# The seam between two layers: four expert blocks in the tile-by-tile end, and the third tile's norm at a lower priority

## The chip, the core and the metric

The kernel runs on one core of a Trainium2 chip. The core has a tensor engine (PE) for matmuls and transposes, VectorE (DVE), ScalarE (ACT) and GpSimd (POOL) for elementwise work, and SyncE (SP), which here only issues DMA transfers. Each engine takes its instructions in a fixed order and waits on semaphores for the others. Matmuls write PSUM, which has 8 banks here; everything else lies in SBUF. The metric is the device time of one execution in microseconds (us); the time before is the median of three runs.

## What is computed

Two layers of a hybrid trunk act on 256 latent tokens and 256 context tokens of width 1024. In each layer one input projection feeds four mixers (a convolution over 31 taps, neighbourhood attention, a Hyena convolution and a Mamba-2 scan), an output projection and a norm follow, then an expert layer (PEER) and a second norm. Cut to the part that matters:

```
for l in range(DEPTH):                                   # DEPTH = 2
    y, yc = mixer_sublayer(x * (1 + sc1) + sh1, xc * (1 + sc1c) + sh1c, ...)
    x = layer_norm(alpha * x + g1 * y, ln1_g[l], ln1_b[l])
    x = layer_norm(alpha * x + g2 * peer(x * (1 + sc2) + sh2, ...), ln2_g[l], ln2_b[l])
    # the same for the context xc, in layer 0 only
```

`peer` weighs the rows of a table of 16384 experts (`peer_v`) for every token and sums them. `mixer_sublayer` of layer 1 begins with `h @ w_in`, and h needs the second norm of layer 0: that step from one layer to the next is the seam.

## The kernel before

**Tiles and blocks.** Tokens stand in tiles of 128. In layer 0 three tiles (0 and 1 latent, 2 context; `DT`) go through a dense form of the expert sum: the 16384 experts are 128 blocks of 128, and for every block the tile's weights (w, made into wh and wl) are multiplied with the block's rows of the value table (v_hi and v_lo). Each product is three matmuls (`mm3`, L144 to L146: hi*hi, hi*lo, lo*hi), for two halves of 512 columns; so a block has 3 x 2 x 3 = 18 matmuls, and the sums lie in six PSUM banks (`ov`). The fourth tile (the other context tile, `GT`) goes another way (gathered rows) and is done before the seam.

**A block's values.** `values` issues one 512 KB transfer into a raw buffer of pool `vp` (SP, v_raw, L1294), casts it on ACT (v_hi, L140) and takes the rest on DVE (v_lo, L141). `VB[0]` is 2: two raw buffers, and two each of v_hi and v_lo. So a block's transfer can be issued once v_lo of two blocks earlier has read the raw buffer, and its v_hi can be written once PE is done with the values of two blocks earlier.

**The end of the expert layer.** The main loop runs the blocks one by one, all three tiles each. The last `NE` blocks are the tail: tile after tile, half after half, with the blocks innermost, so that a tile's sums are complete before the next tile's begin. Then `combine` multiplies a tile's sums with a gate (cm, L1317), adds them to the residual (L1318, one half on DVE, one on POOL), takes statistics (L1319), works out the scale ln_rs (DVE L297, L299; POOL L300 to L302) and applies it on ACT (x_n, L1333). `to_hT` transposes x_n on PE in 2 x 4 steps (xT, L792), scales it into h (ACT L798, DVE L800) and splits that into hT (ACT cast L140, DVE rest L141), the right-hand side of layer 1's projections.

**What comes next.** Layer 1 loads blocks of weights (`load_w`: w_raw; w_hi on ACT L140; w_lo on POOL L141; three buffers each of w_hi and w_lo) and multiplies each with hT (`projT`, banks `pj`, 24 matmuls a block). The first ten blocks use 256 columns, tiles 0 and 1, the later ones with 512 all four tiles. The convolution's input is written to a padded buffer upad (L378), which POOL has cleared (MEMSET, L349); its 31 taps for each of two halves run on DVE (L366 the first, L368 the other 60). The Hyena part's short convolutions (hv: ACT L343, DVE L344, L345) end in a product (L389), which PE transposes (ut, L404). Later the step sizes of the scan are worked out on DVE (L443 to L458, ending with av), which PE needs for pc (L463); then follow the rope products (rot on PE L484; kr, qr, r1k on DVE L486 to L488).

**What sets the order.** A scheduler orders every engine's instructions when the kernel is built, by the dependences, its own estimate of the times and a priority number: work written later has a higher number and goes later, where it can. `low(n)` adds n to that number for what is inside; the taps have low(3000). `tc.issue_after` holds instructions behind a named one. On the chip each engine then runs its list in order.

Of the kernel before, what the change touches and what calls it, by code (L numbers as in the profile page):

```python
# [31 lines left out]
HB2 = 4  # L32
# [9 lines left out]
XB = (96, 100, 104, 108)  # L42
VD = (10, 1)
UM = ((0, 2, 4, 6, 7), (0, 1, 2, 3, 4, 5, 6, 7))
NE = 2
WHB = (4, 5)
WB = 3
PW = (1, 1)
# [38 lines left out]
def tile_hybrid_diffusion(ctx: ExitStack, tc: tile.TileContext, I: dict, out: bass.AP):  # L87
    nc = tc.nc
    V, S, G, T = nc.vector, nc.scalar, nc.gpsimd, nc.tensor
# [723 lines left out]
    prep = {}  # L813
# [33 lines left out]
    for l in range(2):  # L847
# [426 lines left out]
        with ExitStack() as vst:  # L1274
# [17 lines left out]
            def values(bl, p, n, eng=G):  # L1292
                raw = mk(vp, [128, D], tag="v_raw", bufs=VB[l])
                late["v", bl] = nc.sync.dma_start(raw, I["v"][l, bl])  # L1294
                hi = mk(p, [128, D], F32R, tag="v_hi", bufs=n)
                lo = mk(p, [128, D], F32R, tag="v_lo", bufs=n)
                split(raw, hi, lo, eng)
                return hi, lo
# [75 lines left out]
                nc.gpsimd.dma_start(xd[t], x_)  # L1374

            gat = gathered() if GT else iter(())
            last = 128 - NE
            for st in range(UBl, last + UBl):
                if st < 128:
                    u_stage(st)  # L1380
# [11 lines left out]
            ws, vs_ = [], []  # L1392
            for bl in range(last, 128):
                ws.append(weights(bl))
                if bl < 127 or l:
                    vs_.append(values(bl, vp, VB[l], V))
            rg_s.close()
            xp_s = ExitStack()
            x_n = mk(pool("xp", stack=xp_s, side="right"), [128, len(DT), D], name="x_n")
            fle = ExitStack()  # L1400
            if l == 0:
                vs_.append(values(127, pool("vep", stack=fle, side="right"), 1, V))
            end = tc.issue_after(late["v", 127 - VD[l]].ins)
            end.__enter__()
            for i, t in enumerate(DT):
# [20 lines left out]
            end.__exit__(None, None, None)  # L1426
            if l == 0:
                prep.clear()
                prep.update(raw=(pool("fl", stack=fle, side="right"), 3))
            for i, t in enumerate(DT):  # L1430
                for hh in range(2):
                    with tc.issue_after(prev.ins):
                        for j in range(NE):
                            ins = accum(last + j, i, *ws[j], *vs_[j], (hh,))
                    prev = ins
                if i == len(DT) - 1 - FI and l == 0:
                    fill_to(1, FX)
                lst = mk(gp, [128, 1, 2, 6], tag="ln_st")
                r = x_n[:, i, :]
                combine(t, r, gb[t // 2], lambda hh: pacc[i, hh], lst, lnr if l else None)  # L1440
                if l == 0:
                    to_hT([t], lambda t: x_n[:, DT.index(t), :], lnc, hT, gp, hb=HB2)
            fle.close()
        dn.close()
    xp_s.close()
# [116 lines left out]
```

## Time and profile before

| | |
|---|---|
| median of three runs (lowest to highest) | 2890.71 us (2876.44 to 2892.68) |
| the profiled execution, its own time | 2900.05 us |
| its span, mean granted PE clock | 2898.2 us, 0.964 |
| PE busy | 2676.9 us (92%) |
| DVE busy | 2015.2 us (70%) |
| ACT busy | 1122.6 us (39%) |
| POOL busy | 620.0 us (21%) |

All times in the rows below are microseconds from the start of that execution's span. A row gives the start, the length, the engine, the line of the kernel and the operation with the tiles it writes and reads; in brackets stands how long the engine was idle before it and what ended the wait. PE's matmuls overlap: each lasts 0.39 us while the next one starts 0.23 us later. The seam lies between about 1790 and 1940 us.

### The profile page before, as it was taken

Reading aid. Unit: us, or ns where it says so; the run is one execution under the profiler, and the core shown is the slowest. Engines: PE = TensorE matmul, PEld = TensorE weight load, DVE = VectorE, ACT = ScalarE, POOL = GpSimd, SP = SyncE. Lnnn points to the kernel's source line nnn. Section 1 sums busy time; section 2 is a strip of 40 time slices with the busy share of each in tenths; the row PEclk is TensorE's granted clock in tenths of the full one; section 3 lists DMA queues with packets and bytes.
Section 4 is the critical chain, followed back from the end, with each engine's and each line's share of the span. In section 5 each row is a group of like instructions: output and inputs, shape, how many; then the busy total and the mean of one; then the engine's idle time right before and its main releaser. Section 6 shows DMA issues by size and latency. Waiting matters only on the chain. (4 is left out here: it accounts for less than half of the span.)

```text
span 2898.2 us, 41581 instructions
## 1 busy us (share of the span) xinstructions
PE 2676.9 (92%) x15550; PEld 2281.7 (79%) x15550; DVE 2015.2 (70%) x4273; ACT 1122.6 (39%) x1762; POOL 620.0 (21%) x439
## 2 busy tenths in 40 slices
PE   6797899888899999999899999699999999999997
PEld 3674566668889998888788887675889999999986
DVE  4956447968587787877767745875789765555556
ACT  2233531225433333333333333434336544444443
POOL 2233000025423444444334301530000000000000
PEclk8899999989999999999999999799999999999999
DMA  7122333346798999989889835326338976766655
GB/s 258 58 92 95 124 139 102 122 148 248 250 334 310 325 324 321 320 303 307 307 311 312 271 100 182 113 88 218 131 121 306 348 223 203 218 216 200 195 189 197
DMA packets 241838, 625.06 MB, mean 216 GB/s; under 512 B 22424, under 2 KB 104794, under 8 KB 236004
## 3 DMA queue, kind: packets, MB, share of 16 engines
q1 hardware_dynamic: 201156, 475.05, 49.4%
q0 software_dynamic: 40480, 147.36, 14.2%
q8 instruction: 122, 2.00, 0.3%
q14 instruction: 80, 0.66, 0.1%
HBM read 573.04 MB, written 49.30 MB: 215 GB/s over the span
## 5 line engine op out<-in xcount | busy, mean ns | idle before, releaser
L146 PE MATMUL au<-hT,u_lo 128*128 128x384 f32 (+1 forms) x1952 | 612.2, 314 | 19.4 <-POOL u_lo L141 13.8
L144 PE MATMUL au<-hT,u_hi 128*128 128x384 f32 (+1 forms) x1952 | 613.6, 314 | 4.0 <-DVE slT L1212 3.0
L145 PE MATMUL au<-hT,u_hi 128*128 128x384 f32 (+1 forms) x1952 | 610.7, 313 | 0.0
L145 PE MATMUL ov<-v_lo,wh 128*128 128x512 f32 x1280 | 505.5, 395 | 30.0 <-DVE v_lo L141 29.9
L146 PE MATMUL ov<-v_hi,wl 128*128 128x512 f32 x1280 | 501.0, 392 | 0.0
L144 PE MATMUL ov<-v_hi,wh 128*128 128x512 f32 x1280 | 461.9, 393 | 5.8 <-ACT wh L140 5.8
L140 ACT CAST u_hi<-u_raw 128x1024 fp32r<-128x1024 f32 x244 | 256.1, 1050 | 492.7 <-PE au L145 327.7
L146 PEld LDWEIGHTS au<-hT,u_lo 128*128 128x128 f32 x1952 | 371.5, 190 | 24.3 <-POOL u_lo L141 14.8
L144 PEld LDWEIGHTS au<-hT,u_hi 128*128 128x128 f32 x1952 | 371.9, 191 | 12.2 <-DVE slT L1212 3.4
L141 DVE TENSOR_TENSOR u_lo<-u_raw,u_hi 128x1024 fp32r<-128x1024 f32 x220 | 268.4, 1221 | 159.5 <-ACT u_hi L140 159.3
L145 PEld LDWEIGHTS au<-hT,u_hi 128*128 128x128 f32 x1952 | 371.7, 190 | 7.3
L141 DVE TENSOR_TENSOR v_lo<-v_raw,v_hi 128x1024 fp32r<-128x1024 f32 x255 | 312.4, 1226 | 77.7 <-ACT v_hi L140 77.0
L140 ACT CAST v_hi<-v_raw 128x1024 fp32r<-128x1024 f32 x256 | 268.0, 1047 | 112.5 <-DMA v_raw<-in_v_dram 85.2
L145 PEld LDWEIGHTS ov<-v_lo,wh 128*128 128x128 f32 x1280 | 242.0, 189 | 85.1 <-DVE v_lo L141 41.4
L140 ACT CAST wh<-act 128x384 fp32r<-128x384 f32 (+1 forms) x256 | 116.9, 459 | 447.1 <-PE ov L145 444.0
L144 PEld LDWEIGHTS ov<-v_hi,wh 128*128 128x128 f32 x1280 | 242.7, 190 | 50.6 <-ACT wh L140 6.1
L146 PEld LDWEIGHTS ov<-v_hi,wl 128*128 128x128 f32 x1280 | 241.9, 189 | 49.7
L1344 POOL DMA_INDIRECT grow<-in_vg_dram,eu x128 | 179.2, 1400 | 220.7 <-DVE accg L1357 172.0
L1357 DVE SCALAR_TENSOR_TENSOR accg<-grow,ag,accg 128x1024 f32<-128x1024 f32 x127 | 162.8, 1282 | 90.0 <-DMA grow<-in_vg_dram,eu 89.3
L1344 POOL DMA_INDIRECT grow<-in_ug_dram,eu x128 | 163.4, 1276 | 260.9 <-DVE grow L1348 225.9
L141 DVE TENSOR_TENSOR wl<-act,wh 128x384 fp32r<-128x384 f32 (+1 forms) x256 | 125.0, 490 | 101.8 <-ACT wh L140 100.5
L1348 DVE SCALAR_TENSOR_TENSOR grow<-grow,h2n 128x1024 f32<-128x1024 f32 x128 | 155.9, 1221 | 55.3 <-DMA grow<-in_ug_dram,eu 55.2
(834 smaller groups left out, 4039.1 us busy)
## 6 DMA issues: line engine op xcount, KB each, us to landing
u_raw<-in_uT_dram SPq DMA_DIRECT2D x256, 512.0 KB
v_raw<-in_v_dram SPq DMA_DIRECT2D x256, 512.0 KB
Gd<-stg SPq DMA_DIRECT2D x40, 1024.0 KB
gt<-Gd SPq DMA_DIRECT2D x80, 512.0 KB
wa_raw<-in_w_ada_dram SPq DMA_DIRECT2D x76, 512.0 KB
w_raw<-in_w_in_t_dram SPq DMA_DIRECT2D x44, 512.0 KB
w_raw<-in_wq_dram SPq DMA_DIRECT2D x32, 512.0 KB
w_raw<-in_w_ada_dram SPq DMA_DIRECT2D x20, 512.0 KB
```

Source lines behind the costliest of these rows:

```text
L140: S.copy(hi, src)
L141: late["V" if eng in (None, V) else "G"] = (eng or V).tensor_tensor(lo, src, hi.bitcast(F32), ALU.subtract)
L144: T.matmul(o, lh, rh, start=first, stop=False)
L145: T.matmul(o, lh, rl, start=False, stop=False)
L146: return T.matmul(o, ll, rh, start=False, stop=last)
L1344: nc.gpsimd.indirect_dma_start(out=r, out_offset=None, in_=I[tab], in_offset=bass.IndirectOffsetOnAxis(ap=eu[:, i:i + 1], axis=0))
L1348: V.scalar_tensor_tensor(r, r, 1.0, h2n, op0=ALU.mult, op1=ALU.mult, accum_out=ag[:, i:i + 1])
L1357: V.scalar_tensor_tensor(accg, r, ag[:, i:i + 1], accg, op0=ALU.mult, op1=ALU.add)
```

## The change

`NE` becomes a pair: four tail blocks in layer 0, two in layer 1 as before. Of these four, the hi and lo parts of the last two (blocks 126 and 127) lie in pool `vep`, which has two buffers now where it had one for block 127; their raw parts stay in `vp`. Pool `fl` is declared with two buffers where it had three; no tile is taken from it. And for the third tile of layer 0 `combine` and `to_hT` stand in `low(2000)`.

```diff
@@ -42,7 +42,7 @@
 XB = (96, 100, 104, 108)
 VD = (10, 1)
 UM = ((0, 2, 4, 6, 7), (0, 1, 2, 3, 4, 5, 6, 7))
-NE = 2
+NE = (4, 2)
 WHB = (4, 5)
 WB = 3
 PW = (1, 1)
@@ -1374,7 +1374,7 @@
                 nc.gpsimd.dma_start(xd[t], x_)
 
             gat = gathered() if GT else iter(())
-            last = 128 - NE
+            last = 128 - NE[l]
             for st in range(UBl, last + UBl):
                 if st < 128:
                     u_stage(st)
@@ -1392,14 +1392,16 @@
             ws, vs_ = [], []
             for bl in range(last, 128):
                 ws.append(weights(bl))
-                if bl < 127 or l:
+                if bl < 126 or l:
                     vs_.append(values(bl, vp, VB[l], V))
             rg_s.close()
             xp_s = ExitStack()
             x_n = mk(pool("xp", stack=xp_s, side="right"), [128, len(DT), D], name="x_n")
             fle = ExitStack()
             if l == 0:
-                vs_.append(values(127, pool("vep", stack=fle, side="right"), 1, V))
+                vep = pool("vep", stack=fle, side="right")
+                for bl in (126, 127):
+                    vs_.append(values(bl, vep, 2, V))
             end = tc.issue_after(late["v", 127 - VD[l]].ins)
             end.__enter__()
             for i, t in enumerate(DT):
@@ -1426,20 +1428,21 @@
             end.__exit__(None, None, None)
             if l == 0:
                 prep.clear()
-                prep.update(raw=(pool("fl", stack=fle, side="right"), 3))
+                prep.update(raw=(pool("fl", stack=fle, side="right"), 2))
             for i, t in enumerate(DT):
                 for hh in range(2):
                     with tc.issue_after(prev.ins):
-                        for j in range(NE):
+                        for j in range(NE[l]):
                             ins = accum(last + j, i, *ws[j], *vs_[j], (hh,))
                     prev = ins
                 if i == len(DT) - 1 - FI and l == 0:
                     fill_to(1, FX)
                 lst = mk(gp, [128, 1, 2, 6], tag="ln_st")
                 r = x_n[:, i, :]
-                combine(t, r, gb[t // 2], lambda hh: pacc[i, hh], lst, lnr if l else None)
-                if l == 0:
-                    to_hT([t], lambda t: x_n[:, DT.index(t), :], lnc, hT, gp, hb=HB2)
+                with low(2000 if l == 0 and t == DT[-1] else 0):
+                    combine(t, r, gb[t // 2], lambda hh: pacc[i, hh], lst, lnr if l else None)
+                    if l == 0:
+                        to_hT([t], lambda t: x_n[:, DT.index(t), :], lnc, hT, gp, hb=HB2)
             fle.close()
         dn.close()
     xp_s.close()
```

The change moves rows at three places.

PE, where the tail begins, the sums of tile 0's first half (ov_6491): before, with blocks 126 (v_hi_14630) and 127 (v_hi_14651), and the begin of the second half (ov_6495):

```order
L144 MATMUL ov_6491<-v_hi_14630,wh_14624 128x512
L145 MATMUL ov_6491<-v_lo_14631,wh_14624 128x512
L146 MATMUL ov_6491<-v_hi_14630,wl_14625 128x512
L144 MATMUL ov_6491<-v_hi_14651,wh_14637 128x512
L145 MATMUL ov_6491<-v_lo_14652,wh_14637 128x512
L146 MATMUL ov_6491<-v_hi_14651,wl_14638 128x512
L144 MATMUL ov_6495<-v_hi_14630,wh_14624 128x512
L145 MATMUL ov_6495<-v_lo_14631,wh_14624 128x512
L146 MATMUL ov_6495<-v_hi_14630,wl_14625 128x512
```

and of the change, with blocks 124 (v_hi_14568), 125 (v_hi_14581), 126 (v_hi_14609) and 127 (v_hi_14615):

```order
L144 MATMUL ov_6491<-v_hi_14568,wh_14562 128x512
L145 MATMUL ov_6491<-v_lo_14569,wh_14562 128x512
L146 MATMUL ov_6491<-v_hi_14568,wl_14563 128x512
L144 MATMUL ov_6491<-v_hi_14581,wh_14575 128x512
L145 MATMUL ov_6491<-v_lo_14582,wh_14575 128x512
L146 MATMUL ov_6491<-v_hi_14581,wl_14576 128x512
L144 MATMUL ov_6491<-v_hi_14609,wh_14588 128x512
L145 MATMUL ov_6491<-v_lo_14610,wh_14588 128x512
L146 MATMUL ov_6491<-v_hi_14609,wl_14589 128x512
L144 MATMUL ov_6491<-v_hi_14615,wh_14595 128x512
L145 MATMUL ov_6491<-v_lo_14616,wh_14595 128x512
L146 MATMUL ov_6491<-v_hi_14615,wl_14596 128x512
```

The first group has twelve matmuls instead of six and needs four blocks' values. Its end, and with it the second half's begin, stands behind block 127 in both.

POOL, where the padded buffer is cleared (MEMSET upad), between the lo parts of layer 1's weights; before, in front of the fourth of these (w_lo_15008):

```order
L301 TENSOR_TENSOR ln_rs_14845<-ln_rs_14845,nhalf_67 128x1
L141 TENSOR_TENSOR w_lo_14975<-w_raw_14972,w_hi_14974 128x1024
L302 TENSOR_TENSOR ln_rs_14845<-ln_rs_14845 128x1
L349 MEMSET upad_14896 128x572
L141 TENSOR_TENSOR w_lo_15008<-w_raw_15005,w_hi_15007 128x1024
```

and of the change, behind the twelfth (w_lo_15341):

```order
L141 TENSOR_TENSOR w_lo_15253<-w_raw_15250,w_hi_15252 128x1024
L141 TENSOR_TENSOR w_lo_15295<-w_raw_15292,w_hi_15294 128x1024
L141 TENSOR_TENSOR w_lo_15341<-w_raw_15338,w_hi_15340 128x1024
L349 MEMSET upad_14896 128x572
L141 TENSOR_TENSOR w_lo_15387<-w_raw_15384,w_hi_15386 128x1024
```

The MEMSET has moved behind nine more of them.

DVE, around the first write to that buffer (L378); before:

```order
L141 TENSOR_TENSOR hT_2588_14659<-h_14856,hT_2587_14658 128x4x128
L141 TENSOR_TENSOR hT_2588_14659<-h_14868,hT_2587_14658 128x4x128
L150 TENSOR_SCALAR t2k_14905<-t2k_14905 128x256
L378 TENSOR_TENSOR upad_14896<-pj_14945,t2k_14905 128x256
L366 TENSOR_SCALAR yT_14887<-upad_14896,sm_85 128x256
L368 SCALAR_TENSOR_TENSOR yT_14887<-upad_14896,sm_85,yT_14887 128x256 x6
L150 TENSOR_SCALAR t2k_14971<-t2k_14971 128x256
L368 SCALAR_TENSOR_TENSOR yT_14887<-upad_14896,sm_85,yT_14887 128x256 x2
L378 TENSOR_TENSOR upad_14896<-pj_15011,t2k_14971 128x256
L368 SCALAR_TENSOR_TENSOR yT_14887<-upad_14896,sm_85,yT_14887 128x256
```

and of the change:

```order
L141 TENSOR_TENSOR hT_2588_14623<-h_14856,hT_2587_14622 128x4x128
L150 TENSOR_SCALAR t2k_14905<-t2k_14905 128x256
L150 TENSOR_SCALAR t2k_14971<-t2k_14971 128x256
L800 TENSOR_SCALAR h_14868<-xT_14863,lnc_6435 128x128 x2
L141 TENSOR_TENSOR hT_2588_14623<-h_14868,hT_2587_14622 128x4x128
L344 SCALAR_TENSOR_TENSOR hv_14898<-pj_15043,sm_85,hv_14898 128x255
L378 TENSOR_TENSOR upad_14896<-pj_14945,t2k_14905 128x256
L378 TENSOR_TENSOR upad_14896<-pj_15011,t2k_14971 128x256
L344 SCALAR_TENSOR_TENSOR hv_14898<-pj_15085,sm_85,hv_14898 128x255
L345 SCALAR_TENSOR_TENSOR hv_14898<-pj_15043,sm_85,hv_14898 128x255
L366 TENSOR_SCALAR yT_14887<-upad_14896,sm_85 128x256
L344 SCALAR_TENSOR_TENSOR hv_14898<-pj_15128,sm_85,hv_14898 128x255
```

Before, the two writes stood among the first taps, and the short convolutions (hv) came after. Now both halves of tile 2's h (h_14856, h_14868) stand apart, the second one, its hT and one L344 stand directly before L378, and the short convolutions go before the taps. The last tap (L368) stands, before, ahead of the step sizes; in the change the taps go on up to the rope products (L486), and the step sizes' last rows, ending with av, come behind the lo parts of two more projections (w_lo_15784, w_lo_15835). Before:

```order
L454 TENSOR_SCALAR dt_2731_15583<-dt_2731_15583 128x32
L455 TENSOR_TENSOR dt_2731_15583<-dt_2731_15583,dt_2729_15581 128x32
L456 TENSOR_TENSOR dt_15580<-dt_15580,dt_2731_15583 128x32
L458 SCALAR_TENSOR_TENSOR av_15585<-dt_15580,nA_15584 128x32
L141 TENSOR_TENSOR w_lo_15784<-w_raw_15781,w_hi_15783 128x1024
L487 TENSOR_TENSOR kr_15591<-kT_14904,rope_15588 128x256
L486 TENSOR_TENSOR r1k_15729<-rot_15727,rope_15588 128x256
L488 TENSOR_TENSOR kr_15591<-kr_15591,r1k_15729 128x256
L141 TENSOR_TENSOR w_lo_15835<-w_raw_15832,w_hi_15834 128x1024
L487 TENSOR_TENSOR qr_15590<-qT_14903,rope_15588 128x256
L466 TENSOR_TENSOR dsd_15587<-dt_15580,ec_15586 128x4x4 x2
```

and of the change, first where the lo parts stand:

```order
L454 TENSOR_SCALAR dt_2731_15583<-dt_2731_15583 128x32
L368 SCALAR_TENSOR_TENSOR yT_14887<-upad_14896,sm_85,yT_14887 128x256 x2
L453 TENSOR_TENSOR dt_2731_15583<-dt_2731_15583,dt_2730_15582 128x32
L141 TENSOR_TENSOR w_lo_15784<-w_raw_15781,w_hi_15783 128x1024
L368 SCALAR_TENSOR_TENSOR yT_14887<-upad_14896,sm_85,yT_14887 128x256
L487 TENSOR_TENSOR kr_15591<-kT_14904,rope_15588 128x256
L368 SCALAR_TENSOR_TENSOR yT_14887<-upad_14896,sm_85,yT_14887 128x256
L454 TENSOR_SCALAR dt_2731_15583<-dt_2731_15583 128x32
L368 SCALAR_TENSOR_TENSOR yT_14887<-upad_14896,sm_85,yT_14887 128x256
L486 TENSOR_TENSOR r1k_15729<-rot_15727,rope_15588 128x256
L141 TENSOR_TENSOR w_lo_15835<-w_raw_15832,w_hi_15834 128x1024
L453 TENSOR_TENSOR dt_2731_15583<-dt_2731_15583,dt_2730_15582 128x32
L487 TENSOR_TENSOR qr_15590<-qT_14903,rope_15588 128x256
```

Taps stand between them up to here, and the step sizes (L453, L454) are still under way. Some ten rows later av follows:

```order
L454 TENSOR_SCALAR dt_2731_15583<-dt_2731_15583 128x32
L455 TENSOR_TENSOR dt_2731_15583<-dt_2731_15583,dt_2729_15581 128x32
L456 TENSOR_TENSOR dt_15580<-dt_15580,dt_2731_15583 128x32
L458 SCALAR_TENSOR_TENSOR av_15585<-dt_15580,nA_15584 128x32
L466 TENSOR_TENSOR dsd_15587<-dt_15580,ec_15586 128x4x4 x2
L584 TENSOR_TENSOR xdd_15886<-xsn_15577,dsd_15587 128x256
```

So what stood behind av, the lo parts and most of the rope products, now stands ahead of it. On PE the order around pc is the same in both: the matmul that reads av stands ahead of the projection after it.

## Rows read from the trace of the kernel before

**Rows 1.** Windows of 10 us: busy us (x instructions) by engine, granted clock, DMA share.

```profile
core 0: us, PE busy (x) PEld busy (x) DVE busy (x) ACT busy (x) POOL busy (x), PEclk, DMA share, GB/s
...
1810.00:1820.00 10.00, 3.75 (x16) 2.99 (x16) 6.54 (x13) 7.72 (x11) 9.64 (x10) 0.59 0.34 96
...
1860.00:1870.00 10.00, 1.70 (x8) 1.08 (x6) 10.00 (x22) 1.72 (x2) 2.34 (x1) 0.82 0.41 131
1870.00:1880.00 10.00, 4.82 (x13) 3.89 (x14) 10.00 (x26) 0.37 (x1) 0.00 (x0) 0.50 0.00 0
```

**Rows 2.** Timeline of PE at the seam (columns in its first line).

```profile
start us, us, engine line op out<-in xcount [idle before <-releaser]
...
1799.98 0.39 PE L144 MATMUL ov<-v_hi,wh 128*128 128x512 f32 x1
...
1801.60 0.39 PE L144 MATMUL ov<-v_hi,wh 128*128 128x512 f32 x1
...
1808.35 0.40 PE L146 MATMUL ov<-v_hi,wl 128*128 128x512 f32 x1
...
1824.30 1.97 PE L792 MATMUL xT<-cm,x_n 128*128 128x128 f32 x8 [4.27 <-ACT x_n L1333]
1825.92 0.99 PE L144 MATMUL pj<-hT,w_hi 128*128 128x256 f32 x3
```

**Rows 3.** Timeline of DVE at the tail.

```profile
1793.29 1.23 DVE L141 TENSOR_TENSOR v_lo<-v_raw,v_hi 128x1024 fp32r<-128x1024 f32 x1 [0.39 <-ACT v_hi L140]
...
1799.75 1.22 DVE L141 TENSOR_TENSOR v_lo<-v_raw,v_hi 128x1024 fp32r<-128x1024 f32 x1 [1.34 <-ACT v_hi L140]
1801.80 0.69 DVE L1317 TENSOR_TENSOR cm<-ov,gb 128x512 f32<-128x512 f32 x1 [0.82 <-PE ov L146]
```

**Rows 4.** Timeline of ACT at the tail.

```profile
1796.10 1.05 ACT L140 CAST v_hi<-v_raw 128x1024 fp32r<-128x1024 f32 x1 [2.84 <-PE ov L146]
1798.67 1.05 ACT L140 CAST v_hi<-v_raw 128x1024 fp32r<-128x1024 f32 x1 [1.52 <-DMA v_raw<-in_v_dram]
...
1810.23 1.24 ACT L1333 ACTIVATE x_n<-x_n,ln_rs 128x1024 f32<-128x1024 f32 x1 [8.99 <-POOL ln_rs L302]
```

**Rows 5.** Timeline of POOL at the seam.

```profile
1818.48 2.34 POOL L141 TENSOR_TENSOR w_lo<-w_raw,w_hi 128x1024 fp32r<-128x1024 f32 x1
...
1821.36 0.57 POOL L349 MEMSET upad<- 128x572 f32 x1
...
1854.44 2.41 POOL L141 TENSOR_TENSOR w_lo<-w_raw,w_hi 128x1024 fp32r<-128x1024 f32 x1 [0.24 <-ACT w_hi L140]
```

**Rows 6.** Timeline of DVE from the convolution to the rope products.

```profile
1835.00 0.42 DVE L378 TENSOR_TENSOR upad<-pj,t2k 128x256 f32<-128x256 f32 x1
...
1837.32 11.25 DVE L368 SCALAR_TENSOR_TENSOR yT<-upad,sm,yT 128x256 f32<-128x256 f32 x6
...
1862.69 0.47 DVE L344 SCALAR_TENSOR_TENSOR hv<-pj,sm,hv 128x255 f32<-128x255 f32 x1
...
1878.90 3.63 DVE L368 SCALAR_TENSOR_TENSOR yT<-upad,sm,yT 128x256 f32<-128x256 f32 x9
...
1911.84 2.38 DVE L454 TENSOR_SCALAR dt<-dt 128x32 f32<-128x32 f32 x1
...
1920.13 0.19 DVE L458 SCALAR_TENSOR_TENSOR av<-dt,nA 128x32 f32<-128x32 f32 x1
1920.24 1.23 DVE L141 TENSOR_TENSOR w_lo<-w_raw,w_hi 128x1024 fp32r<-128x1024 f32 x1
...
1924.08 0.25 DVE L466 TENSOR_TENSOR dsd<-dt,ec 128x16 f32<-128x16 f32 x2
...
1931.02 0.42 DVE L486 TENSOR_TENSOR r1k<-rot,rope 128x256 f32<-128x256 f32 x1 [2.80 <-PE rot L484]
```

**Rows 7.** Timeline of PE at ut and pc.

```profile
1875.18 0.66 PE L404 MATMUL ut<-cm,hv 128*128 128x128 f32 x2 [13.48 <-DVE hv L389]
...
1920.38 1.30 PE L463 MATMUL pc<-av,cm 128*128 128x32 f32 x10 [1.09 <-DVE av L458]
```

## What the change is predicted to do

> **What bounds the kernel now.** I read first the page and the windows, then engine by engine the timeline around the seam, 1780 to 1945 us of the profiled execution. Outside the seam the tensor engine (PE) is the bound; here the windows show two places where it is not [rows 1]: from 1810 (3.75 of 10 us busy, granted clock 0.59, a mix of full 2.4 GHz and half 1.2 GHz) and from 1860 to 1880 (1.70 and 4.82 us, clock down to 0.50). The first: the tail's matmuls run from 1799.98, each tile's norm follows on VectorE (DVE), GpSimd (POOL) and ScalarE (ACT); the third tile's transposes come at 1824.30 and layer 1's first projection (pj) at 1825.92 [rows 2], 17.3 us after the last tail matmul (1808.35 + 0.23). The second, 13.48 us, ends with a DVE operation (hv, L389) at 1875.18 [rows 7]: DVE is behind. It stays close to the bound up to 1920.38, where PE waits 1.09 us for av (L458), which DVE began at 1920.13 [rows 6, 7]. So three times settle the seam: when pj starts, when DVE may start its convolution (L378, then the taps L366 and L368), and when DVE reaches av.
>
> **1. Four tail blocks instead of two.** The tail starts 2 x 18 matmuls earlier, at about 1791.8. But tile 0's first group now needs the values of blocks 124 to 127, not of 126 and 127 alone. Those of 125 are ready at 1793.29 + 1.23 = 1794.5 [rows 3]; they reuse a buffer of block 123, as before. Block 126 gains by "vep": its cast waited for PE until 1796.10 [rows 4]. Block 127 doesn't: its raw values go into the raw buffer of 125, so their transfer is issued after 1794.5 in both kernels; the cast waited for it until 1798.67 [rows 4], and v_lo(127) ended at 1799.75 + 1.22 = 1800.97 [rows 3]. PE takes its queue in order, so it stands in front of block 127's matmuls of tile 0 until then, and the first group ends at 1801.60 + 0.23, as now [rows 2]. What follows is 72 - 12 = 60 matmuls instead of 30. From 1801.60 to 1808.35 there are 29 steps of 0.2327 us, so 30 more cost **+6.98 us**. Eight transposes (x_n of tile 0) now stand before the very last tail matmul: 1.97 us for eight at half clock [rows 2], half of that at full, so +1.0 to +1.9. Tail end: 1808.58 + 6.98 + 1.0 to 1.9 = 1816.6 to 1817.5; I take 1817.0.
>
> **2. From the tail's end to pj.** Before, three norm chains queued up behind each other. Now those of tiles 0 and 1 lie beside the 14 us of matmuls, which are their cover; what is left is one chain, the third. Its length by tile 0's: from the first combine (1801.80) to x_n (1810.23) 8.43 us, x_n itself 1.24, transposes to pj 1825.92 - 1824.30 = 1.62 [rows 2, 3, 4]: 11.3 us. Bounds: six matmuls (1.4 us) less, if the chain is counted from the end of its second half; 2.34 us more, since on POOL a w_lo (L141, 2.34 us [rows 5]) stands before the last step of ln_rs (L302). pj starts at 1817.0 + 11.3 = 1828.3, bounds 1816.6 + 9.9 = 1826.5 and 1817.5 + 13.6 = 1831.1. Against 1825.92: **+2.4 us** (+0.6 to +5.2). What the overlap gains on tiles 0 and 1, the wait in the first group spends.
>
> **3. The low priority.** Three of the last four transposes (second half of tile 2) go between the projections, the last after the ninth block of 24 matmuls; DVE's h and hT for them stand in front of L378, and on POOL the MEMSET of upad has moved from 1821.36, ahead of the fourth w_lo, to behind the twelfth. That w_lo ran at 1854.44 for 2.41 us [rows 5] and ended 30.9 us after pj began. So the MEMSET ends at 1828.3 + 30.9 + 0.57 = 1859.8, and L378 starts then, not at 1835.00 [rows 6]: **+24.8 us**. Behind it on DVE's queue stand the other L378, the 62 taps and most of the short convolutions (L344, L345), for which layer 1's banks and PE's ut wait. The second gate (h and hT of tile 2's last half) opens at nearly the same time, since its last transpose follows block nine too; to take either away alone would not free DVE.
>
> What DVE loses is less. From 1835.00 to 1862.69 it did only 22 operations of this work in 27.7 us, because six taps beside POOL's w_lo took 11.25 / 6 = 1.87 us each, while nine without took 3.63 / 9 = 0.40 [rows 6]. Uncontended, 22 cost 22 x 0.41 = 9.0 us; one w_lo (the thirteenth) still falls into them, +1.9. L378 itself took 0.42 us in front of the contended ones. By the Trainium skill (page "SBUF — State Buffer", section "Who interferes with whom") a DVE instruction with two SBUF inputs and a GpSimd instruction that reads SBUF exclude each other for a whole instruction. The trace agrees: 1.87 against 0.40 us; if instead a POOL operation slowed all of DVE's work in proportion, the 22 would be no cheaper later, and av 17 us later still.
>
> **4. To av.** From 1862.69 to 1920.32 DVE did 57.6 us of work, waits of 2.9 us among it. In the new order the work of 1920.24 to 1924.08, 3.84 us [rows 6] (the w_lo of two projections, rope products) stands before av, and so do the last taps; PE's order still has pc (L463), which needs av, ahead of the next projection. av: 1859.8 + 9.0 + 1.9 + 57.6 - 0.5 (one L344 done earlier) + 3.8 = 1931.6, less 0 to 2.9 us of former waits that taps now fill. I take 1.7 of these: 1929.9, against 1920.32: **+9.6 us**, bounds +6.5 (pj early, all waits filled) and +14 (pj late, none). PE waited there already, so it has no slack, although it comes to its ut (L404) earlier: L389 is done some 20 operations after L378, 1859.8 + 20 x 0.41 + 1.9 = 1870 against 1875.18. Those 5 us are given back at pc.
>
> **5. After pc** PE runs pj and rot in turns up to 1938; DVE's wait of 2.80 us at 1931.02 [rows 6] shows that DVE follows PE there, and in the new order most of its work for that stretch is done before. So what arrives at pc is passed on to the end; the main loop and all of layer 1's experts are unchanged. Sum: +9.6 us, rounded **+10 us**. The profiled execution took 2900.05 us (span 2898.2), which makes 2910 by its own time; the median of the three runs, 2890.71, is 9.3 us below it, and I state the time against the median: **2901 us**.
>
> **The rivals.**
> *Faster: DVE makes it all up.* After 1862.69 POOL's long operations also stretch some of DVE's small ones (the one at 1911.84 took 2.38 us [rows 6]; five such cost about 10 us over their 0.4). If these now meet no DVE operation of that kind, all waits vanish and pj starts at its lower bound, av is 10 + 1.2 + 1.8 = 13 us earlier than summed, 3 us earlier than before, and PE keeps this out of its 5 us won at ut: 2888 us; with the whole 5, 2886. It decides where the work from L378 to av shrinks from 70 us to below 60. Against it: the taps now also run in this stretch, so there is more for POOL to meet, not less. Chance 0.13.
> *About the same.* Half of those 10 us vanish: +4.6, 2895 us. Chance 0.2.
> *Slower.* In the first group of the tail PE works 0.7 us and waits about 2, three times between 1792.5 and 1801.0. After the idle 13.48 us of the trace the clock was at half, and the 4.82 us that PE then worked in 1870:1880 at 0.50 [rows 1, 7] would have been 2.4 at full. If the clock falls here, the tail loses as much; pj, MEMSET and av shift by that; with pj at its upper bound (+2.8) and no waits filled (+1.7): 9.6 + 6.9 = +16.5, 2907 us. It decides where the tail ends after 1819. Chance 0.17. The Trainium skill ("TensorE: Matmul & The Clock Gate", "What's actually happening") says that the array's clock drops to 1.2 GHz after idleness; the trace agrees for the pause of 13.48 us; no row shows what three of 2 us do.
> *The change doesn't do what it says.* That tile 0 can't finish earlier than now is in the forecast; that the low priority moves nothing that waits would need av hidden, against which stands PE's wait of 1.09 us: 2891 us, within the two first.
>
> **How the numbers follow.** The forecast has 0.5 (+6 to +14 us, 2897 to 2905), the rivals 0.13, 0.2 and 0.17. The range from 2883 to 2915 takes in 2886 and 2907 and leaves out less than 2 in 10, mostly for runs that differ as those shown do (2876.44 to 2892.68). Some 1% (28.9 us) is what a measurement of this kernel can tell from no change. All cases lie within it: the sum with every bound at its worst gives some 20 us, and the largest gain, both holes of PE closed, 17.3 + 13.5 = 31 us. Faster by over 1% 0.01, within 0.95, slower by over 1% 0.04.
>
> **What would show it.** Right: PE stands in tile 0's first group until about 1801; x_n of tile 0 near 1810; pj at 1827 to 1831; L349 ending near 1860 and L378 right behind it, its taps at 0.4 us; ut near 1870; PE's wait at L463 some 10 us or more instead of 1.09. Wrong: v_lo(127) before 1800, pj before 1826, the MEMSET before 1850, or av before 1924.

## The result, and the profile after

The changed kernel takes 2908.62 us (median of 8 runs, 2897.97 to 2916.87) where the kernel before, in as many runs beside it, takes 2891.1: a ratio of 1.0065, 95% interval 1.0046 to 1.0083, some 17 to 19 us slower. That is inside the predicted range and within 1%, but nearly twice the +10 us of the sum, and outside the forecast's own band (+6 to +14 us, 2897 to 2905). The profiled execution took 2908.7 us (span 2906.9, clock 0.965).

The spans can't be subtracted as they stand: layer 0 before the seam took 6.9 us less in this execution, and it varied by more than that between profiles of one kernel. So every time below that is called an offset counts from the start of v_hi (L140) of the 120th block (block 119, since they count from 0), 1769.01 before and 1762.07 after:

```profile
1762.07 1.05 ACT L140 CAST v_hi<-v_raw 128x1024 fp32r<-128x1024 f32 x1
...
1787.10 1.05 ACT L140 CAST v_hi<-v_raw 128x1024 fp32r<-128x1024 f32 x1 [0.74 <-DMA v_raw<-in_v_dram]
1791.75 1.04 ACT L140 CAST v_hi<-v_raw 128x1024 fp32r<-128x1024 f32 x1 [3.60 <-DMA v_raw<-in_v_dram]
```

(ACT's timeline of the changed kernel; the last two casts are those of blocks 126 and 127, each waiting for its transfer.) From there to the end of the span it is 1129.2 us before and 1144.8 after, +15.6.

| offset, us | v_lo(127) ends | pj | L378 | ut | pc | cmu (L758) | pot (L966) |
|---|---|---|---|---|---|---|---|
| before | 31.97 | 56.91 | 65.99 | 106.17 | 151.36 | 174.31 | 254.45 |
| after | 31.98 | 60.15 | 93.06 | 104.95 | 162.81 | 187.93 | 270.40 |
| difference | 0.0 | +3.2 | +27.1 | -1.2 | +11.5 | +13.6 | +15.9 |

(Starts, except for v_lo. cmu is the next stage's first matmul behind layer 1's projections, pot its output projection. Past pot the difference of these two stays; in other executions it changes there by up to 2.9 us.) The windows of the changed kernel, against [rows 1]:

```profile
core 0: us, PE busy (x) PEld busy (x) DVE busy (x) ACT busy (x) POOL busy (x), PEclk, DMA share, GB/s
...
1790.00:1800.00 10.00, 7.16 (x24) 5.03 (x23) 4.00 (x5) 1.04 (x1) 0.40 (x1) 0.67 0.96 383
...
1810.00:1820.00 10.00, 1.88 (x14) 1.33 (x12) 8.01 (x15) 9.97 (x19) 5.50 (x6) 0.85 0.04 6
...
1840.00:1850.00 10.00, 10.00 (x86) 10.00 (x85) 0.00 (x0) 3.34 (x4) 8.18 (x4) 1.00 0.57 165
...
1860.00:1870.00 10.00, 6.25 (x26) 4.85 (x25) 10.00 (x18) 2.24 (x4) 3.27 (x2) 0.91 0.42 131
...
1910.00:1920.00 10.00, 0.80 (x6) 0.40 (x4) 10.00 (x18) 1.32 (x2) 4.75 (x2) 0.80 0.05 11
1920.00:1930.00 10.00, 5.12 (x25) 5.12 (x26) 5.42 (x22) 0.30 (x1) 2.38 (x4) 0.52 0.27 93
```

PE's hole between 1860 and 1880 of before has nearly closed. A new one stands at 1910 to 1925, and in 1840:1850 DVE does nothing at all: it waits at its gate while PE works, and later PE waits while DVE is fully busy. PE's timeline shows the same places:

```profile
1792.84 0.79 PE L144 MATMUL ov<-v_hi,wh 128*128 128x512 f32 x1 [2.37 <-ACT v_hi L140]
1794.10 0.79 PE L145 MATMUL ov<-v_lo,wh 128*128 128x512 f32 x1 [0.47 <-DVE v_lo L141]
1794.70 0.63 PE L146 MATMUL ov<-v_hi,wl 128*128 128x512 f32 x1
...
1796.40 0.47 PE L144 MATMUL ov<-v_hi,wh 128*128 128x512 f32 x1
...
1809.51 1.04 PE L792 MATMUL xT<-cm,x_n 128*128 128x128 f32 x8
1810.30 0.48 PE L146 MATMUL ov<-v_hi,wl 128*128 128x512 f32 x1
...
1821.24 1.33 PE L792 MATMUL xT<-cm,x_n 128*128 128x128 f32 x5 [9.24 <-ACT x_n L1333]
1822.22 0.56 PE L144 MATMUL pj<-hT,w_hi 128*128 128x256 f32 x1
...
1867.02 0.41 PE L404 MATMUL ut<-cm,hv 128*128 128x128 f32 x2 [3.75 <-DVE hv L389]
...
1924.88 2.34 PE L463 MATMUL pc<-av,cm 128*128 128x32 f32 x10 [14.08 <-DVE av L458]
1927.04 0.56 PE L144 MATMUL pj<-hT,w_hi 128*128 128x256 f32 x1
```

Against [rows 7]: the wait of 13.48 us at ut is down to 3.75, the one of 1.09 at pc up to 14.08, and the ten matmuls of pc take 2.34 us instead of 1.30. DVE and POOL, against [rows 5, 6]:

```profile
1850.96 0.41 DVE L800 TENSOR_SCALAR h<-xT,lnc 128x128 f32<-128x128 f32 x1 [14.01 <-PE xT L792]
...
1853.79 1.01 DVE L141 TENSOR_TENSOR hT<-h,hT 128x512 fp32r<-128x512 f32 x1 [1.18 <-ACT hT L140]
...
1855.12 0.74 DVE L378 TENSOR_TENSOR upad<-pj,t2k 128x256 f32<-128x256 f32 x2
...
1858.78 2.44 DVE L368 SCALAR_TENSOR_TENSOR yT<-upad,sm,yT 128x256 f32<-128x256 f32 x1
...
1861.53 0.47 DVE L368 SCALAR_TENSOR_TENSOR yT<-upad,sm,yT 128x256 f32<-128x256 f32 x1
...
1864.61 2.26 DVE L389 TENSOR_TENSOR hv<-hv 128x256 f32<-128x256 f32 x1
...
1905.08 5.18 DVE L368 SCALAR_TENSOR_TENSOR yT<-upad,sm,yT 128x256 f32<-128x256 f32 x2
...
1924.63 0.19 DVE L458 SCALAR_TENSOR_TENSOR av<-dt,nA 128x32 f32<-128x32 f32 x1
```

```profile
1851.89 2.37 POOL L141 TENSOR_TENSOR w_lo<-w_raw,w_hi 128x1024 fp32r<-128x1024 f32 x1 [0.49 <-ACT w_hi L140]
1854.20 0.58 POOL L349 MEMSET upad<- 128x572 f32 x1
...
1858.54 2.39 POOL L141 TENSOR_TENSOR w_lo<-w_raw,w_hi 128x1024 fp32r<-128x1024 f32 x1 [3.76 <-ACT w_hi L140]
...
1864.25 2.34 POOL L141 TENSOR_TENSOR w_lo<-w_raw,w_hi 128x1024 fp32r<-128x1024 f32 x1 [3.32 <-ACT w_hi L140]
...
1905.01 9.74 POOL L939 TENSOR_TENSOR x_n<-x_n,lnr 128x1024 f32<-128x1024 f32 x4 [18.23 <-DMA lnr<-in_lnr_dram]
```

The MEMSET stands behind the twelfth w_lo, and the second L378 follows the first within 0.33 us. DVE's wait of 14.01 us ended with the last transpose (xT); the hT behind it ended at 1854.80 and the MEMSET at 1854.78, so both gates of L378 opened together.

### The profile page after: what moved, and what is told of

Same layout as the page of the kernel before. It is cut to its first block, busy times and chain, and to the rows that moved or that the text cites. A ratio compares the mean times of both kernels' runs of the same rounds, so it can differ in the third digit from the quotient of the medians.

```text
span 2906.9 us, 41574 instructions
## 1 busy us (share of the span) xinstructions
PE 2680.8 (92%) x15550; PEld 2284.6 (79%) x15550; DVE 2012.9 (69%) x4273; ACT 1122.2 (39%) x1762; POOL 590.6 (20%) x439
## 4 chain that ended last, share of the span: by engine, by line
PE 39%; DMA 13%; issue 10%; DVE 10%; POOL 5%; ACT 1%; SPq 0%; POOLq 0%; DVEq 0%; ACTq 0%
DMA grow<-in_vg_dram,eu 7%; PE ov L145 5%; PE ov L144 5%; PE ov L146 5%; PE au L144 5%; PE au L146 5%; PE au L145 5%; POOL grow L1344 5%; DMA gt<-Gd 2%; DMA grow<-in_lnr_dram 2%; DVE accg L1357 2%; PE au L1017 1%; DVE yT L368 1%; PE G L1248 1%; PE G L1249 1%
## 5 line engine op out<-in xcount | busy, mean ns | idle before, releaser
L140 ACT CAST u_hi<-u_raw 128x1024 fp32r<-128x1024 f32 x244 | 256.1, 1050 | 471.9 <-PE au L145 326.2
L146 PEld LDWEIGHTS au<-hT,u_lo 128*128 128x128 f32 x1952 | 370.6, 190 | 11.7 <-DVE u_lo L141 10.3
L140 ACT CAST v_hi<-v_raw 128x1024 fp32r<-128x1024 f32 x256 | 267.9, 1047 | 111.3 <-DMA v_raw<-in_v_dram 82.2
L140 ACT CAST wh<-act 128x384 fp32r<-128x384 f32 (+1 forms) x256 | 116.9, 459 | 456.4 <-PE ov L145 456.4
```

Of the source, the lines that this page charges most:

```text
L140: S.copy(hi, src)
L146: return T.matmul(o, ll, rh, start=False, stop=last)
```

## The experiments

The theory to test (A): the four blocks cost a few microseconds at pj, the low priority delays L378 and with it av, and pc, in PE's queue ahead of projections that could run, hands DVE's delay to PE. All offsets are differences to the first profile of before, as in the table above. One kernel's own spread sets what they can tell: two profiles of before differ by up to 2.2 us in them, so less than that between two kernels says nothing alone.

| kernel | v_lo(127) | pj | L378 | ut | pc | cmu | pot | ratio of times (95%) |
|---|---|---|---|---|---|---|---|---|
| changed | 0.0 | +3.2 | +27.1 | -1.2 | +11.5 | +13.6 | +15.9 | 1.0065 (1.0046 to 1.0083) |
| after_again | -0.1 | +4.4 | +27.4 | -0.9 | +11.8 | +14.9 | +18.3 | one execution |
| before_again | -0.5 | -1.9 | -2.2 | -2.2 | -2.2 | -2.2 | -2.2 | one execution |
| four_blocks | -0.4 | +3.3 | +6.5 | +3.4 | +5.9 | +5.9 | +10.1 | 1.0032 (1.0012 to 1.0052) |
| low_combine | -0.2 | +3.8 | +2.2 | +3.1 | +3.1 | +3.1 | +6.2 | 1.0026 (1.0007 to 1.0046) |
| pc_later | -0.2 | +4.0 | +26.8 | -1.5 | moved | +2.5 | +7.3 | 1.0018 (0.9997 to 1.0038) |
| pc_later_before | -0.3 | -1.9 | -1.8 | -1.8 | moved | -3.2 | -7.2 | 1.0005 (0.9982 to 1.0029) |
| own_raw | -1.7 | +3.0 | +26.1 | -2.2 | +10.5 | +13.7 | +17.5 | 1.0063 (1.0041 to 1.0084) |
| four_own_raw | -1.8 | +1.9 | +5.1 | +1.9 | +2.8 | +2.8 | +4.8 | 1.0020 (1.0001 to 1.0039) |
| four_own_raw_pc | -2.2 | 0.0 | +3.2 | -0.1 | moved | -0.4 | +3.3 | 1.0030 (1.0011 to 1.0049) |
| split_raw | -0.6 | +4.0 | +2.5 | +3.4 | +3.3 | +3.3 | +8.4 | 1.0029 (1.0013 to 1.0045) |
| split_raw_pc | -0.5 | +3.2 | +2.8 | +3.7 | moved | +2.3 | +4.3 | 1.0011 (0.9993 to 1.0030) |

**four_blocks**: four tail blocks, the usual priority.

```diff
-                with low(2000 if l == 0 and t == DT[-1] else 0):
+                with low(0):
```

> The change without its low priority: four tail blocks alone. Its lists have the MEMSET of upad behind the fourth w_lo and the taps ahead of the short convolutions, nearly as before; three of the last transposes still go into the first projections. Theory A (the low priority's place for L378 makes DVE late, and PE pays for it at pc): the tail and the begin of pj are as in the change, some 3 us late against before; L378 starts 3 to 4 us late, not 27; PE waits 0 to 3 us at pc, not 14; the seam is longer than before by 3 to 4 us, 2894 to 2895 us. Theory B (the four blocks themselves cost it: the wait in tile 0's first group and the clock that falls with it are carried to the end): the seam stays 14 to 16 us longer than before, 2905 to 2908 us.

2895.70 against 2888.36 us. cmu came 5.9 us later, so of the +13.6 of the changed kernel 7.7 go with the low priority; the times agree (0.33% between the two ratios, 9.5 us). The four blocks alone cost more than A's 3 to 4 us: without the low priority, too, the MEMSET moved, here behind the fourth w_lo, and three transposes of the third tile went in among the first projection's matmuls, so that hT, which also took 2.88 us here, and L378 came later. POOL's and DVE's timelines:

```profile
1833.31 0.58 POOL L349 MEMSET upad<- 128x572 f32 x1
```

```profile
1833.96 2.88 DVE L141 TENSOR_TENSOR hT<-h,hT 128x512 fp32r<-128x512 f32 x1
1836.77 0.41 DVE L378 TENSOR_TENSOR upad<-pj,t2k 128x256 f32<-128x256 f32 x1
```

L378 waited for hT here, not for the MEMSET, done 2.9 us before. By ut this delay had gone (+3.4, as at pj). The other 2.6 us came up between ut and pc, where PE waited 2.0 us at pdn (L422; 0.6 before) and the granted clock was 0.50 from 1902 to 1904. low_combine, with four blocks too, has none of them (+3.1 at ut and at pc), so they needn't belong to the four blocks.

**low_combine**: the low priority around `combine` alone, `to_hT` behind it at the usual one.

```diff
-                    if l == 0:
-                        to_hT([t], lambda t: x_n[:, DT.index(t), :], lnc, hT, gp, hb=HB2)
+                if l == 0:
+                    to_hT([t], lambda t: x_n[:, DT.index(t), :], lnc, hT, gp, hb=HB2)
```

> The change with the low priority around the third tile's combine alone, its transposes and h at their usual place: all transposes stand ahead of the first projection, the MEMSET behind the third w_lo and L378 right behind the last hT, as before; only the four tail blocks differ from before. Theory A (what the low priority cost lies in where h and the MEMSET stand): pj +3.3 to +3.7 us against before, L378, ut and pc by the same, cmu +3.7, the seam +4 to +8 with the clock after cmu; 2892 to 2896 us. Rival (the four blocks delay DVE by more than pj, as in the run without low priority, +5.9 at cmu): +6 to +10, 2895 to 2899 us.

2899.74 against 2889.70 us, cmu +3.1: A's number for cmu, not the rival's. All transposes stand ahead of pj again and the MEMSET (at 1819.59 in its profile) ahead of the fourth w_lo, and from ut to cmu the difference is constant: PE waits 13.49 us at ut and 1.09 at pc, as before. So what the low priority does, it does through `to_hT`: with it alone out of its reach, 10.5 of the 13.6 us at cmu are gone. The ratios of the times, 1.0065 and 1.0026, are 11 us apart, which agrees. The time itself missed both expectations: by the medians it is 10.0 us above before; 3.1 us more were lost between cmu and pot, a stretch that is spoken of below.

**pc_later**: the changed kernel, but in layer 1 `ssd_ec()`, which issues pc, is called one projection later.

```diff
-            if m == 0:
+            if m == 0 and not l:
                 ssd_ec()
...
             S.copy(vn[:, :, m * 128:(m + 1) * 128], b.rearrange("p (t c) -> p t c", c=128))
+            if m == 0 and l:
+                ssd_ec()
```

> The change with pc (L463) written two projections later in layer 1, so that on PE the next projections no longer stand behind its wait for av; DVE's list stays as it is, late taps and all. Theory A: PE goes on with the two projections at once or as soon as their lo parts (DVE, 5 to 7 us before av in the change) are there; its wait of 14.08 us at pc shrinks to below 7 in sum over this stretch, the clock has less time to fall; the seam is 5 to 11 us longer than before instead of 15.9, 2896 to 2902 us. Theory B, or DVE itself being the bound through here: the wait moves to the next matmul that needs DVE (a lo part, xdd or the conformer's norm), the seam stays within 2 us of 15.9, 2906 to 2910 us.

2894.92 against 2888.36 us, a little below A's 2896. L378 and av are as late as in the changed kernel (+26.8, av +12.0), yet cmu is only 2.5 us later: 11.1 us regained by the place of one step in PE's queue. PE's timeline of it:

```profile
1905.11 0.80 PE L146 MATMUL pj<-hT,w_lo 128*128 128x512 f32 x1 [4.11 <-DVE w_lo L141]
...
1912.96 1.20 PE L463 MATMUL pc<-av,cm 128*128 128x32 f32 x10
1913.99 0.47 PE L144 MATMUL pj<-hT,w_hi 128*128 128x512 f32 x1
```

pc now waits for nothing; what remains is a wait of 4.11 us for a w_lo that DVE makes.

**pc_later_before**: the same edit in the kernel before (two blocks, no low priority).

> The kernel before, two tail blocks and no low priority, but ssd_ec() of layer 1 called after the first vT projection, as in pc_later. Theory A (pc passes DVE's delay on to PE, and that alone is what pc_later regained): before, PE waited 1.09 us at pc, so at most about 1 us is regained: cmu -1.5 to +0.5 against the kernel before, the time within 0.1% of it. Rival (the later place is by itself the better order of PE's queue, whatever DVE does): cmu -4 us or more, the time 0.15% lower, and then a version faster than both kernels.

2887.75 against 2887.85 us: the same time. cmu -3.2 lies between the two expectations, but the seam was 1.9 us early in this execution from pj on (as in before_again, -2.2 throughout); what is left, 1.3, is close to the 1.09 us that PE waited at pc. So the later place is no gain in itself; it regained what the changed kernel had made pc cost.

**own_raw**: the changed kernel with the raw values of blocks 126 and 127 in buffers of their own.

```diff
-                raw = mk(vp, [128, D], tag="v_raw", bufs=VB[l])
+                raw = mk(p, [128, D], tag="v_raw", bufs=n)
```

> The change with raw buffers of their own for the values of blocks 126 and 127, so that block 127's transfer no longer waits for v_lo of block 125. Theory A: the first group of tile 0 ends earlier by up to 6 us (it still waits for block 125, ready some 2.7 us after the tail starts, and for the casts of 126 and 127 behind it); pj, the MEMSET behind the twelfth w_lo, L378, av and pc all come earlier by the same amount, since each hangs on pj; the seam is 10 to 12 us longer than before, 2901 to 2903 us. Rival: the transfers, not the buffers, are the limit (they follow each other on the queues): the last lands only 1 to 2 us earlier, 2906 to 2908 us.

2905.74 against 2888.36 us: no better than the changed kernel, and A missed. v_lo(127) was only 1.7 us earlier: a transfer's issue on SP waited 5.7 us for a wl of the main loop, so the new buffers seem to lie in memory that it still used (concluded from this wait, not shown apart). SP's waits, 1750 to 1780, and PE's timeline:

```profile
SPq L1294 <- DVE wl L141: 5.7, 1, 5.7
```

```profile
1781.26 0.75 PE L144 MATMUL ov<-v_hi,wh 128*128 128x512 f32 x1 [1.64 <-ACT v_hi L140]
1782.52 0.80 PE L145 MATMUL ov<-v_lo,wh 128*128 128x512 f32 x1 [0.51 <-DVE v_lo L141]
1783.11 0.63 PE L146 MATMUL ov<-v_hi,wl 128*128 128x512 f32 x1
...
1787.38 0.63 PE L144 MATMUL ov<-v_hi,wh 128*128 128x512 f32 x1
```

From 1783.11 to 1787.38 ten steps took 0.427 us each, at a granted clock of 0.50 (1782 to 1788); at the 0.233 of [rows 2] they are 1.9 us shorter. The tail's last matmul was 8.7 us late (8.9 in the changed kernel): the clock took back most of what the buffers won.

**four_own_raw**: four_blocks with these buffers.

> Four tail blocks without the low priority and with own raw buffers for blocks 126 and 127. Theory A: the tail loses most of its wait and the norms of two tiles lie beside it, so pj starts 2 to 4 us earlier than before and what follows keeps the order of before: the seam is 1 to 4 us shorter than before, 2887 to 2890 us. Theory B (four blocks cost by themselves): 5 us or more longer than before, above 2896 us. If the gain at pj is lost again, DVE, which is full from L378 on, takes it: 2891 us.

2894.45 against 2888.36 us; cmu +2.8 against four_blocks' +5.9, pj +1.9. Both theories missed. At pj it is better than four_blocks by 1.4 us, about its earlier v_lo(127); the rest is what four_blocks lost between ut and pc. It is still behind before.

**split_raw**: low_combine with a raw buffer of its own for block 126 alone.

```diff
-                raw = mk(vp, [128, D], tag="v_raw", bufs=VB[l])
+                raw = mk(p if bl == 126 and l == 0 else vp, [128, D], tag="v_raw", bufs=1 if bl == 126 and l == 0 else VB[l])
```

> As the run with the low priority around combine alone, with a raw buffer in vep for block 126 alone; block 127's raw values then go into block 124's buffer, so that their transfer waits for v_lo of block 124, 4.1 us earlier than that of 125 and 2.5 us earlier than for the memory that it met with own buffers for both. Theory A: v_lo of block 127 ends 3.5 to 4.2 us earlier than in the change, PE waits some 3 us in tile 0's first group instead of 7, and its clock has no time to fall; the tail ends 4 to 6 us earlier than in the change, pj lies at -1 to -2.5 us against before, cmu too; the seam -2 to +3, 2886 to 2891 us. Rival (another wait takes its place, as with own buffers for both): pj still +2 to +3, 2892 to 2895 us.

2900.55 against 2889.70 us, v_lo(127) only 0.6 us earlier, cmu +3.3: the rival's case, with pj (+4.0) and the time above its numbers. On SP a transfer waited 2.1 us for a wl; that it was block 126's, ahead of 127's in the same queue, is concluded from the edit.

**split_raw_pc**: split_raw with pc later. **four_own_raw_pc**: four_own_raw with pc later.

> As the run before it, with pc written two projections later. PE waited 1.09 us at pc in the kernel before; if that wait is all that pc costs there, this gains 1 us at cmu against the run before it (2885 to 2890 us); if the next use of DVE's results waits instead, nothing.

> Four tail blocks at the usual priority, raw buffers of blocks 126 and 127 of their own, and ssd_ec() of layer 1 after the first vT projection. Theory A (what is left is the later start of pj, and pc has little left to pass on): pj +1.9, cmu +1.5 to +3, about as four_own_raw (+2.8), the time 0.1 to 0.25% above before. Rival (the wait at pc still holds some microseconds that PE could have used): cmu below +0.5, the time at or below that of before.

2892.62 against 2889.70 us, and 2894.08 against 2887.85. With pc's wait near 1 us (1.02 and 0.92) little is to be regained there: split_raw_pc's cmu is 1.0 us earlier than split_raw's, as expected; that its ratio is 0.18% lower is not explained by this. four_own_raw_pc came 3.2 us ahead of four_own_raw at cmu, into the rival's range, but 1.9 of this stand already at pj, where the two don't differ in their work: in its tail the granted clock stayed at 1.00, while it was 0.50 in 1792:1794 of four_own_raw. Its time is no better. No version beat the kernel before.

**before_again** and **after_again**: each of the two kernels once more, one execution.

> The kernel before, once more, to see how well the seam repeats. From the cast of v_hi of block 120 to layer 1's first query matmul (pq, L1067) it took 281.8 us in the profile of before, 174.3 of these to cmu (L758) and 80.2 from there to the output projection (L966). If the stretch up to cmu is set by the lists alone it repeats within 0.5 us. From cmu on the runs so far took 80.2 to 84.9 us with the same list, the granted clock of the second 10 us being 0.50 to 0.81 among them: if that is chance, this run lies anywhere between 80 and 85; if it belongs to the kernel, it is 80.2 again.

> The changed kernel itself, one more look. Theory (the loss up to cmu, L758, belongs to the order of the work): counted from the cast of block 120, pc comes 10.5 to 12.5 us later than before (11.5 in the first profile), cmu 12.5 to 14.5 (13.6), PE's wait at pc 13 to 15 us. Rival (some of it is how the clock happened to fall): cmu outside of 11.5 to 15.5. For the stretch from cmu to pot (L966), 82.5 us in the first profile against 80.1 twice before: if its length belongs to the kernel, it is within 0.7 us of 82.5; if it goes with where the granted clock happens to change, it may stand anywhere from 80 to 85.

Before repeats within 2.2 us, not within the 0.5 that was expected. Most of it is one DVE operation, here in DVE's timeline of before, then in those of DVE and POOL of before_again:

```profile
1818.55 2.82 DVE L141 TENSOR_TENSOR hT<-h,hT 128x512 fp32r<-128x512 f32 x1 [0.47 <-ACT hT L140]
```

```profile
1805.07 0.69 DVE L141 TENSOR_TENSOR hT<-h,hT 128x512 fp32r<-128x512 f32 x1 [0.17 <-ACT hT L140]
```

```profile
1805.30 2.67 POOL L141 TENSOR_TENSOR w_lo<-w_raw,w_hi 128x1024 fp32r<-128x1024 f32 x1
```

In before this hT began 0.07 us behind POOL's w_lo of 1818.48 [rows 5] and took 2.82 us; in before_again it began 0.23 us ahead of it and took 0.69, as in pc_later_before. The third tile's x_n and pj came 2 us later by it. So the profile from which the prediction was worked out was a late one: against before_again pj of the changed kernel is +5.2, cmu +15.8 and pot +18.1, not +3.2, +13.6 and +15.9.

The changed kernel repeats within 1.2 at pj, 0.3 at pc (14.08 us of wait again) and 1.3 at cmu (+14.9, between the numbers of theory and rival). The stretch from cmu to pot doesn't repeat: 80.1 us in both profiles of before, but 76.1 in pc_later_before, 82.5 and 83.5 in the changed kernel, 82.1 to 85.2 in the other four-block kernels, with the same number of PE's instructions within one. The windows over it, of before_again, pc_later_before and the changed kernel:

```profile
1928.19:2008.33 80.14, 70.40 (x473) 43.40 (x472) 46.53 (x119) 40.01 (x77) 6.06 (x8) 0.89 0.53 180
```

```profile
1934.34:2010.45 76.11, 66.36 (x474) 41.18 (x472) 46.40 (x119) 40.15 (x77) 6.06 (x8) 0.96 0.51 171
```

```profile
1950.00:2032.47 82.47, 70.48 (x473) 44.08 (x472) 46.45 (x119) 39.73 (x77) 6.39 (x8) 0.90 0.51 175
```

Between before_again and pc_later_before the granted clock differs (0.89 and 70.40 us of PE's busy time against 0.96 and 66.36). Between before_again and the changed kernel it doesn't (0.89 and 70.40 against 0.90 and 70.48): their 2.3 us are waits of PE for DVE at yd (L629), 5.9 us in sum instead of 3.7. One of the two waits makes the difference; PE's timeline, before and changed:

```profile
1966.30 0.66 PE L629 MATMUL yd<-t2k,xsn 128*64 128x128 f32 x8 [2.29 <-DVE t2k L624]
```

```profile
1973.74 0.88 PE L629 MATMUL yd<-t2k,xsn 128*64 128x128 f32 x8 [4.56 <-DVE t2k L624]
```

The lists are not the same here, other than before_again's expectation has it. The three profiles with two blocks agree in the order of PE's and DVE's instructions from cmu to pot; in all ten with four blocks it is another one. So the change moved rows at a fourth place, behind the three of the section on the change. Whether this order makes the longer wait was not tested.

The Trainium skill ("TensorE: Matmul & The Clock Gate", "What's actually happening") says that the number of slow matmuls varies from run to run; the two profiles of the two-block order, 76.1 and 80.1, agree. That all ten profiles with four blocks lie above all three with two may be the other order or the clock; it stays open.

## Why the prediction was right, and where it was short

The range (2883 to 2915) held the time because it was wide. The forecast's band did not, and the number next to the result, 2907, is the slower rival's. What held is the mechanism of steps 1 to 4; what the sum missed stands in step 5 and in the profile that it started from.

**Step 1, right.** v_lo(127) ended at offset 31.98, predicted 31.96: block 127's transfer is issued no earlier, so PE stood in the first group until then. The tail's last matmul came 8.9 us later: 6.98 for 30 matmuls, 0.79 for eight transposes ahead of it (forecast 1.0 to 1.9), and about 1.2 that the sum had left out: the granted clock was 0.50 from 1790 to 1796, and behind the waits of 2.37 and 0.47 us the next matmuls ran at it (four steps of 0.427 us from 1794.70 to 1796.40, and a part of two others). This is the slower rival's mechanism, just too small to decide: the tail ended at offset 48.7 (49.8 in after_again, with 0.50 from 1798 to 1806), and the rival needed 50.0 (1819). A small reading of step 1 is off without touching its sum: before, the first group ended at 1801.60, where the second half's first matmul begins, not 0.23 us later.

**Step 2, right.** pj +3.2, predicted +2.4 within 0.6 to 5.2; of the 0.9 that it is later the tail has 0.5 and the norm's chain 0.4 (11.7 us instead of 11.3). Against before_again (+5.2) it is just within the bounds: pj came where it was forecast, but the profile of before had pj 2 us late.

**Step 3, right in its mechanism, 1.4 us short.** L378 came 32.9 us after pj, predicted 31.5: the twelfth w_lo ended 32.0 us after pj instead of 30.9, since the last eight waited 4.0 us in sum for their w_hi on ACT (2.5 before), and L378 then stood behind hT and an L344. That hT, the second gate, opened with the MEMSET, as forecast; no run takes away one of the two alone. The regained speed is there: taps at 0.4 us a piece, and from L378 to the end of av 69.7 us, predicted 70.1, against 85.3 before. But L378 was 2.3 us later than forecast, and two w_lo, not one, fell into the first 22 operations (2.44 and 2.26 us), so that ut came 1.2 us earlier and not 5. (The forecast's 1.87 us a tap was a mean of a merged row: of those six, four took 2.5 us and two 0.5.) By the Trainium skill ("SBUF — State Buffer", "Who interferes with whom") a DVE instruction with two SBUF inputs is held by a GpSimd one that reads SBUF; the trace agrees, 2.44 us for the L368 beside the w_lo of 1858.54 and 0.47 for the next one. That the faster rivals didn't come is the same thing: POOL's L939 from 1905.01 met the taps there (5.18 us for two).

**Step 4, right.** av and pc +11.5, predicted +9.6; the 1.9 us are the 0.9 and 1.4 of steps 2 and 3, less 0.4 from L378 to av. pc_later shows the mechanism: same av, 11.1 us less at cmu.

**Step 5, the step that was short.** "What arrives at pc is passed on to the end" left out what the wait itself does to PE. [Rows 1] and [rows 7] had it: after 13.48 us of idleness the clock stood at 0.50. The forecast made a wait of that length at pc and charged nothing for what follows. In the trace pc's matmuls took 2.34 us instead of 1.30, and pj behind them ran slowly too (its first start-to-start step took 0.36 us instead of 0.20, the next ten 0.21 instead of 0.12; the granted clock was 0.50 up to 1928): 1.0 + 1.2 us, and +11.5 at pc became +13.6 at cmu; after_again repeats it (2.34 us, cmu +14.9). Another 2.3 us came up between cmu and pot: the wait at yd, in a stretch where the forecast expected nothing new; why it is longer is not shown. So +9.6 + 1.9 + 2.1 + 2.3 less 0.3 to the end make the +15.6 of the two profiles. The times say +17.5. The 2 us by which the profile of before was late may be part of the gap; single profiles can't settle it.

Of the parts of the change, the four blocks bring nothing and cost something, 0.20 to 0.32% in the four versions that have them without the late gate and with pc in its place: their first group waits for the last transfer either way, and the matmuls that stood beside that transfer now come after it. The low priority, through `to_hT`, puts the gate of DVE's longest chain behind projections that could have waited.

## What to carry to other kernels

Before more work is put into a tail, look at what its first step waits for: if that is the last transfer, a longer tail ends later by the work added. Work put off on one engine has a price where another engine's queue has a fixed place for its result; count from that place, and try to move it (11 us here) before the work itself. And charge a new wait of PE for the slow matmuls behind it, by the nearest wait of that length in the same trace. Profile the kernel before twice where a few microseconds count: the place of one operation against another engine's was worth 2 us here.

## What the runs showed of the hardware

Several short waits of PE in the midst of dense matmuls were followed by the lower clock in some executions and not in others. In the changed kernel PE waited 0.65, 0.76 and 0.76 us between 1785 and 1790, and the granted clock was 0.50 from 1790 to 1796, through the waits of 2.37 and 0.47 us. In own_raw it waited 0.64, 0.76, 0.16 and 1.64 us, and then ten steps ran at 0.427 us. In four_own_raw_pc the waits at the same place were 3.5 us in sum, and the clock stayed at 1.00 through the tail. In before PE hardly waits in this stretch, since the main loop's matmuls still stand beside the last transfers, and the clock is 1.00 in each window from 1780 to 1810. And one order of the same instructions took from 76.1 to 80.1 us between cmu and pot, with the mean clock at 0.96 and 0.89.

The same DVE operation with two SBUF inputs took 0.69 or 2.82 us in the same kernel, according to whether it began 0.23 us ahead of POOL's w_lo or 0.07 us behind it.
